# The first stage of a hybrid encoder step: another order of loads, norm steps, weight splits and first dense products

## The chip, the cores and the metric

The kernel runs on one core of a Trainium2 chip. The metric is the device time of one execution in microseconds (us). The engines are named as in the profile: PE (TensorE matmul), PEld (its weight loads), DVE (VectorE), ACT (ScalarE), POOL (GpSimd) and SP (SyncE, which issues most transfers).

## The reference

One layer of a streaming encoder is computed for two request groups that share all weights: 1024 prompt rows and 32 sample rows, here laid side by side as T = 1056 columns. Cut to what matters here:

```
h = rms_norm(x, g_pre_mix)                   # over D_MODEL = 1024
z = h @ w_in                                 # GLA q,k,v,r,rank | band q,k,v | gates gA,gB
... two branches, mixed, w_out, ConvFFN ...
gate = sigmoid(rms_norm(x, g_pre_ple) @ w_ple_gate)
x = x + rms_norm(gate * (pe @ w_ple), g_post_ple)
```

The product pe @ w_ple (called PLE below) does not depend on anything else, so the kernel computes it first, while x is still being loaded and normalised.

## The kernel before, in words

All matrices lie with features on the 128 partitions: x is eight blocks of 128 x 1056, loaded as four parts of two blocks each and two column halves, `one` (columns 0 to 527) and `two` (528 to 1055). Every fp32 product is made from three passes over values split in a high and a low part (hi*hi, hi*lo, lo*hi). A split is an ACT copy to the rounded type (hi) and a subtraction (lo).

The program is written out by hand up to the end of the first stage (`manual_schedule`): PE, DVE and ACT each run their instructions in the order in which the code emits them, and an instruction that waits holds all that stands behind it on its engine. SP issues its transfers in the order of its queue in the same way. The stages that matter:

- **Warm-up and loads** (L311 to L355). The first half of the PLE weights, the three column chunks of p (352 columns each), the small vector table, the four parts of half `one` of x, the second half of the PLE weights, the four parts of half `two`, then `war` and `state_conv`.
- **PLE** (the loop over `PLE`, L443 to L463). 24 groups of six matmuls of 352 columns (L230 to L232): three column tiles for each chunk, then five further tiles. After each group the previous one is copied out of PSUM (`evac`, L457 on ACT; the middle chunk by DVE, L455); after the last chunk of a tile SP writes the tile to DRAM (L459, `d_pl`). There are six PSUM buffers for the groups and four SBUF buffers `ev` for the tiles. The table `S` says which steps of the norm are emitted after which group.
- **Norm of a half** (`x_square`, `x_add`, `x_sums`, `x_inverse`, `x_norm`, `x_low`). ACT squares each part (L363, L366), DVE adds the squares up and folds them (L371, L373, L375), two fp32 matmuls with a constant matrix sum over partitions (L382), ACT takes ln and exp (L385, L386), DVE finishes the reciprocal root (L391 to L395), and then, for each part, DVE scales x (L400), ACT makes the high part xh (L401) and DVE the low part xl (L405).
- **First plain products** (`plain_half`, L469 to L483, and `alr_half`). The band q, k and v tiles and a 48-column rank tile, first for half `one`, then for half `two`: eight k steps of six matmuls of 264 columns each (L475 to L477). The weights' low parts are made by POOL (L331 with `eng=po`, L415). Hooks in the first product emit the sums of half `two`.
- **Sums for the dense pairs** (`sum_differences`, `sum_high`, `sum_low`). Differences of x's blocks for the Strassen-like products, made by DVE (L529 to L531, L540) and ACT (L537) while half `two` is multiplied.
- **Dense pairs** (`in_strassen`). Each pair of output tiles is made of seven products of 24 matmuls (L615 to L617) into three PSUM pairs X, Y, Z. The first product goes to X and is copied to `p1` (L626); weight sums come from DVE (L598) and are split by ACT and DVE (L605, L606). From here on the order is chosen by a scheduler.

Everything behind the dense pairs (band attention, linear recurrence, output product, ConvFFN, gate) follows on PE without a gap of its own order; the change does not touch it, and the order there is the same before and after on every engine.

## Time and profile before

| what | us |
|---|---|
| median of three runs | 1961.51 (1960.55 to 1961.64) |
| the profiled execution | 1960.96 |
| its span | 1959.2 |
| first matmul of PLE | 5.23 |
| sums of half one on PE | 21.52 |
| sums of half two on PE | 51.53 |
| first matmul of the first dense pair | 89.87 |

The span is the time from the first to the last instruction, and the profiled execution took 1.76 us more. A row of the timeline gives the start, the duration, the engine, the line and the tiles; in square brackets stands how long the engine was idle before, and which instruction released it. A row of the windows gives, for a stretch of time, the busy time of PE, PEld, DVE, ACT and POOL with the count of instructions, then the granted clock of PE, the busy share of the DMA engines and the GB/s that they moved. Matmuls overlap, so the pace of PE is read from start to start, not from durations.

### The profile page before, as it was taken

What the parts mean: (1) busy time and instruction counts of PE and PEld (TensorE: products, weight loads), DVE (VectorE), ACT (ScalarE), POOL (GpSimd) and SP (SyncE); (2) the same over time, 40 slices, a digit from 0 to 9 for tenths busy, and PEclk for the clock granted to TensorE, in tenths of its full rate; (3) what the DMA queues carried; (4) which work ended last, traced back from release to release, by engine and by line L of the source; (5) the groups of instructions that cost most, each with busy time, mean ns of one, the idle gap of its engine ahead of it and who ended that gap; (6) DMA issues with size and microseconds to landing.
All of it is one profiled execution on the core that took longest, in us unless ns stands there. A gap on an engine that the chain in (4) does not pass through costs nothing.

```text
span 1959.2 us, 34930 instructions
## 1 busy us (share of the span) xinstructions
PE 1901.6 (97%) x13960; PEld 1863.5 (95%) x13960; DVE 1286.2 (66%) x2368; ACT 929.1 (47%) x1812; POOL 219.6 (11%) x359
## 2 busy tenths in 40 slices
PE   7999999999999999999999999999999999999996
PEld 7999999998999999998999999999999999999996
DVE  6855544556556777778544586777767766558776
ACT  6434334666664454443333455433333345555555
POOL 1100001000000101000320111111121211000112
PEclk9999999999999999999999999999999999999998
DMA  6233325233315455567834245543354559897746
GB/s 257 88 105 100 110 87 181 70 90 88 93 47 144 141 132 155 139 180 218 326 132 126 89 154 196 191 145 127 112 135 110 119 142 308 267 296 240 239 155 106
DMA packets 111120, 300.91 MB, mean 154 GB/s; under 512 B 12453, under 2 KB 34797, under 8 KB 110317
## 3 DMA queue, kind: packets, MB, share of 16 engines
q1 hardware_dynamic: 82652, 210.28, 33.8%
q0 software_dynamic: 28016, 88.05, 16.7%
q8 instruction: 109, 1.79, 0.4%
q14 instruction: 55, 0.44, 0.1%
q10 hardware_dynamic: 288, 0.36, 0.1%
HBM read 201.20 MB, written 114.09 MB: 161 GB/s over the span
## 4 chain that ended last, share of the span: by engine, by line
PE 75%; DVE 13%; ACT 7%; issue 3%; DMA 1%; POOL 0%; SPq 0%; ACTq 0%; DVEq 0%; POOLq 0%
PE two L1903 6%; PE two L1905 6%; PE two L1904 6%; PE mm L230 5%; PE mm L232 5%; PE mm L231 5%; PE mm L796 4%; PE mm L798 4%; PE mm L797 4%; PE two L615 4%; PE two L617 3%; PE two L616 3%; PE two L2350 3%; PE two L2349 3%; PE two L2348 3%
## 5 line engine op out<-in xcount | busy, mean ns | idle before, releaser
L796 PE MATMUL mm<-xh,whi 128*128 128x352 f32 x696 | 236.6, 340 | 0.0
L798 PE MATMUL mm<-xh,wlo 128*128 128x352 f32 x696 | 225.4, 324 | 0.0
L797 PE MATMUL mm<-xl,whi 128*128 128x352 f32 x696 | 224.6, 323 | 0.0
L2350 PE MATMUL two<-d,wlo 128*128 128x264 f32 x616 | 175.5, 285 | 1.2 <-DVE wlo L2092 1.2
L2349 PE MATMUL two<-d,whi 128*128 128x264 f32 x616 | 174.7, 284 | 2.0 <-DVE d L2043 2.0
L2348 PE MATMUL two<-d,whi 128*128 128x264 f32 x616 | 174.7, 284 | 0.8 <-ACT d L2042 0.8
L1905 PE MATMUL two<-mh,wlo 128*128 128x264 f32 x576 | 163.0, 284 | 0.0
L1904 PE MATMUL two<-ml,whi 128*128 128x264 f32 x576 | 162.9, 284 | 0.0
L1903 PE MATMUL two<-mh,whi 128*128 128x264 f32 x576 | 161.2, 284 | 0.0
L796 PEld LDWEIGHTS mm<-xh,whi 128*128 128x128 f32 x696 | 131.3, 189 | 1.7
L797 PEld LDWEIGHTS mm<-xl,whi 128*128 128x128 f32 x696 | 131.2, 189 | 0.4
L798 PEld LDWEIGHTS mm<-xh,wlo 128*128 128x128 f32 x696 | 130.5, 187 | 0.0
L2349 PEld LDWEIGHTS two<-d,whi 128*128 128x128 f32 x616 | 115.8, 188 | 2.4 <-DVE d L2043 2.4
L2348 PEld LDWEIGHTS two<-d,whi 128*128 128x128 f32 x616 | 116.4, 189 | 1.1 <-ACT d L2042 1.1
L2350 PEld LDWEIGHTS two<-d,wlo 128*128 128x128 f32 x616 | 115.6, 188 | 1.6 <-DVE wlo L2092 1.6
L1905 PEld LDWEIGHTS two<-mh,wlo 128*128 128x128 f32 x576 | 108.4, 188 | 0.0
L1904 PEld LDWEIGHTS two<-ml,whi 128*128 128x128 f32 x576 | 108.4, 188 | 0.0
L1903 PEld LDWEIGHTS two<-mh,whi 128*128 128x128 f32 x576 | 107.3, 188 | 0.0
L932 ACT ACTIVATE s<-s,sm 128x640 f32<-128x640 f32 (+5 forms) x72 | 50.6, 703 | 97.1 <-DVE sm L931 97.0
L615 PE MATMUL two<-th,whi 128*128 128x264 f32 x320 | 91.0, 284 | 0.0
L1893 ACT ACTIVATE whi<-ws 128x512 fp32r<-128x512 f32 x72 | 45.2, 631 | 96.4 <-PE two L1904 71.4
L616 PE MATMUL two<-tl,whi 128*128 128x264 f32 x320 | 90.9, 284 | 0.0
(610 smaller groups left out, 6009.2 us busy)
## 6 DMA issues: line engine op xcount, KB each, us to landing
raw<-in_w_in SPq DMA_DIRECT2D x52, 512.0 KB, 3.8
uraw<-d_b SPq DMA_DIRECT2D x34, 528.0 KB, 4.7
d_b<-av POOLq DMA_DIRECT2D x33, 528.0 KB, 4.0
d_ws<-in_w_down POOLq DMA_DIRECT2D x24, 704.0 KB, 6.5
raw<-in_w_up SPq DMA_DIRECT2D x27, 512.0 KB, 3.7
wraw<-d_ws SPq DMA_DIRECT2D x16, 704.0 KB, 6.5
d_b<-gc POOLq DMA_DIRECT2D x11, 792.0 KB, 5.0
sraw<-in_w_up SPq DMA_DIRECT2D x17, 512.0 KB, 4.7
```

Of the source, the lines that this page charges most:

```text
L230: pe.matmul(ps, h, xh(kt), start=(first and i == 0), stop=False)
L615: pe.matmul(ps[:, j, :HC], w[0][:, k], x[0](k, s), start=st, stop=False, skip_group_check=True)
L616: pe.matmul(ps[:, j, :HC], w[0][:, k], x[1](k, s), start=False, stop=False, skip_group_check=True)
L796: pe.matmul(ps, wh, h[:, k, s], start=(k == 0), stop=False)
L797: pe.matmul(ps, wh, l[:, k, s], start=False, stop=False)
L798: pe.matmul(ps, wl, h[:, k, s], start=False, stop=(k == cnt - 1))
L1903: pe.matmul(ps[:, j, :HC], w[0][:, k], x[0][:, k, s], start=st, stop=False, skip_group_check=True)
L1904: pe.matmul(ps[:, j, :HC], w[0][:, k], x[1][:, k, s], start=False, stop=False, skip_group_check=True)
L1905: pe.matmul(ps[:, j, :HC], w[1][:, k], x[0][:, k, s], start=False, stop=sp_, skip_group_check=True)
L2348: pe.matmul(o, wh, xh_[:, s], start=(k == 0 and p in (0, 4, 5)), stop=False, skip_group_check=True)
L2349: pe.matmul(o, wh, xl_[:, s], start=False, stop=False, skip_group_check=True)
L2350: pe.matmul(o, wl, xh_[:, s], start=False, stop=(k == HD - 1 and p in (3, 4, 6)), skip_group_check=True)
```

## The change

Five things change in the first stage.

1. **Loads.** The parts of x's half `one` are loaded between the parts of p. The first w_in tile (QB0) is loaded ahead of half `two`.
2. **Norm steps.** The table `S` is laid out anew, x_norm and the copy to xh are separate steps (`x_norm`, `x_high`), and the steps of half `two` are spread over the three plain products by a table `N`.
3. **No POOL splits.** All low parts of weights come from DVE. All 24 PSUM copies of PLE go to ACT, and the eight writes of PLE tiles (`d_pl`) are issued by ACT and no longer by SP. Two tiles use a buffer of their own (`z`).
4. **Half two** multiplies its tiles in the order 2, 0, 1, and the sums for the dense pairs are emitted in another order.
5. **First dense pair.** Its weights are loaded and the two that need no sum (a11, a12) are split during half `two`; the pair then starts with a11*b11 and a12*b21, both into X.

```
-    x_load(one)
+    x_load(one, 0)
     for c in (1, 2):
         for kt in range(2):
             dma.dma_start(pin[:, kt, chunk(c)], a["p"][kt, :, chunk(c)])
+        x_load(one, 2 * c)
+    x_load(one, 6)
...
-            acc[h.start] = tl(st, [P, 2, HT], tag="acc", bufs=2)
+            acc[h.start] = tl(st, [P, 2, HT], tag="acc", bufs=1)
...
-            wfirst[n] = next(raw_split(raws[n], eng=po))
+            wfirst[n] = next(raw_split(raws[n]))
...
-        po.tensor_tensor(l, raws[n], h, op=ALU.subtract)
+        ve.tensor_tensor(l, raws[n], h, op=ALU.subtract)
...
+    first_load(0)
+    for i in range(0, KT, 2):
+        x_load(two, i)
...
-         9: [lambda: x_square(one, 3)], 10: [lambda: x_add(one, 3), lambda: x_sums(one)],
+         9: [lambda: x_add(one, 3)], 10: [lambda: wple.append(next(raw_split(raws[1]))), lambda: first_load(1)], 11: [lambda: x_sums(one)],
...
-                zs[n] = evt()
-            if c == 1:
-                ve.tensor_copy(zs[n][:, s], ps)
-            else:
-                ac.activation(zs[n][:, s], ps, AF.Copy)
+                zs[n] = tl(st, [P, T], tag="z", bufs=1) if n % 5 == 1 else evt()
+            ac.activation(zs[n][:, s], ps, AF.Copy)
             if c == NC - 1:
-                dma.dma_start(d_pl[n], zs[n])
+                ac.dma_start(d_pl[n], zs[n])
...
+    N = {(0, 0): [lambda: x_low(one, 3), alr_weights, lambda: x_square(two, 3)], (0, 2): [lambda: x_add(two, 2), lambda: first_split(3)],
+         (0, 4): [lambda: x_add(two, 3)], (1, 0): [lambda: first_split(4)], (1, 1): [lambda: x_sums(two)],
...
+    def early_split(n, b):
+        early[n] = [tl(wp, [P, HK, P], F32R, tag=t, bufs=4) for t in ("whi", "wlo")]
+        split_hi_lo(*early[n], early["raw"][0][:, b])
...
+    for i, n in enumerate((2, 0, 1)):
+        plain_half(n, two, sum_hook(i))
     alr_half(two)
+    early_split("a12", up2)
+    sum_low(0, 1)
...
-        mul(X, weight(a11), "b11", True, True)
+        mul(X, early.pop("a11", None) or weight(a11), "b11", True, True)
         ac.activation(p1, X_, AF.Copy)
+        lead = early.pop("a12", None)
+        if lead:
+            mul(X, lead, "b21", False, True)
+            ac.activation(c11, X_, AF.Copy)
```

Where it moves instructions. ACT's queue of before, from the copy of the third PLE group to the ln of half one (`ev` are PLE tiles, `sq` squares of x, `whi` the high part of the second PLE weights; waits in brackets):

```order
L457 ACTIVATE ev_219<-mm_201 128x352
L363 ACTIVATE acc_229<-xr_113 128x1056
L366 ACTIVATE sq_239<-xr_114 128x1056
L457 ACTIVATE ev_195<-mm_241 128x352
L366 ACTIVATE sq_259<-xr_113 128x1056
L330 ACTIVATE whi_261<-raw_151 128x512
L330 ACTIVATE whi_265<-raw_151 128x512
L457 ACTIVATE ev_208<-mm_250 128x352
L457 ACTIVATE ev_219<-mm_271 128x352
L366 ACTIVATE sq_290<-xr_114 128x1056
L457 ACTIVATE ev_299<-mm_281 128x352
L385 ACTIVATE y_303<-one_304 128x264
```

ACT's queue of the changed kernel from the square of x's last part of half one on:

```order
L363 ACTIVATE sq_262<-xr_114 128x1056 [waits DMAHW5_49,DVE_49]
L458 ACTIVATE z_206<-mm_252 128x352 [waits PE_49]
L460 DMA d_pl_88<-z_206 128x1056 [waits DMAHW0_49,Activation_49]
L458 ACTIVATE ev_217<-mm_264 128x352 [waits PE_49]
L460 DMA d_pl_88<-ev_217 128x1056 [waits DMAHW1_49,Activation_49]
L458 ACTIVATE ev_291<-mm_273 128x352 [waits PE_49]
L330 ACTIVATE whi_293<-raw_151 128x512
L330 ACTIVATE whi_297<-raw_151 128x512
L458 ACTIVATE ev_291<-mm_284 128x352 [waits PE_49]
L382 ACTIVATE y_311<-one_312 128x264 [waits PE_49]
```

The writes of PLE tiles now stand in ACT's own queue. The kernel has eight semaphores for SP's and ACT's transfers (DMAHW0 to DMAHW7), given out in turn, so each write waits for the transfer that had the semaphore eight transfers earlier. A little further on in the same queue, behind exp:

```order
L458 ACTIVATE ev_291<-mm_303 128x352
L460 DMA d_pl_88<-ev_291 128x1056 [waits DMAHW3_49,Activation_49]
L360 ACTIVATE acc_328<-xr_113 128x1056 [waits DVE_49]
L458 ACTIVATE ev_337<-mm_319 128x352 [waits PE_49]
L458 ACTIVATE ev_337<-mm_330 128x352 [waits PE_49]
L363 ACTIVATE sq_354<-xr_114 128x1056 [waits DMAHW2_49]
L458 ACTIVATE ev_337<-mm_344 128x352 [waits PE_49]
L460 DMA d_pl_88<-ev_337 128x1056 [waits DMAHW4_49,Activation_49]
L400 ACTIVATE xh_111<-xr_113 128x2x528 [waits DVE_49]
```

DMAHW3 and DMAHW4 are the semaphores of the third and fourth part of x's half `two`; the first high part xh stands behind both writes. On PE, the start of the first dense pair in the changed kernel (`whi_860` is a11, `whi_947` is a12, `two_974` is X; the rows left out repeat the three passes):

```order
L618 MATMUL two_974<-xh_111,whi_860 128x264 [waits DVE_49]
L619 MATMUL two_974<-xl_112,whi_860 128x264
L620 MATMUL two_974<-xh_111,wlo_861 128x264
...
L618 MATMUL two_974<-xh_111,whi_947 128x264 [waits Activation_49]
L619 MATMUL two_974<-xl_112,whi_947 128x264
L620 MATMUL two_974<-xh_111,wlo_948 128x264 [waits DVE_49]
...
L618 MATMUL two_1029<-th_778,whi_1030 128x264 [waits Activation_49]
```

Before, the second product there was the one with `th` and a summed weight; now a second product into X follows the first.

## The prediction

> **What bounds the kernel now.** I read the page first, then the waits of PE in the first 260 us, the windows of ten microseconds there, the windows around PE's slow stretches, and last the timeline row by row.

> ```profile
> span 1959.2 us, 34930 instructions
> ...
> PE 1901.6 (97%) x13960; PEld 1863.5 (95%) x13960; DVE 1286.2 (66%) x2368; ACT 929.1 (47%) x1812; POOL 219.6 (11%) x359
> ```

> PE is busy 97% of the span, so only a stage in which PE waits or runs slowly can give much. The first stage is one: all PE waits of the first 260 us lie ahead of the first dense pair.

> ```profile
> PE one L382 <- DVE acc L375: 4.9, 1, 4.9
> PE mm L477 <- POOL wlo L331: 1.6, 1, 1.6
> PE two L615 <- DVE ev L495: 1.3, 1, 1.3
> PE mm L475 <- ACT whi L330: 1.2, 1, 1.2
> PE mm L476 <- DVE xl L405: 0.9, 1, 0.9
> PE mm L230 <- ACT ev L457: 0.8, 1, 0.8
> ```

> Next to the waits stands a second loss. PE's clock falls to half after two long idle stretches (columns: busy PE, PEld, DVE, ACT, POOL, then the granted clock):

> ```profile
> 18.37:21.79 3.42, 0.27 (x1) 0.28 (x2) 2.50 (x3) 1.21 (x2) 1.24 (x2) 1.00 1.07 387
> 21.50:25.20 3.70, 3.68 (x11) 3.28 (x12) 1.03 (x2) 1.42 (x3) 0.00 (x0) 0.54 1.04 416
> 45.68:49.10 3.42, 0.60 (x3) 0.30 (x2) 3.28 (x3) 3.30 (x6) 2.06 (x2) 1.00 0.20 79
> 49.10:52.50 3.40, 3.33 (x13) 3.13 (x14) 0.58 (x1) 0.00 (x0) 3.40 (x3) 0.50 0.16 28
> 605.00:607.50 2.50, 0.46 (x6) 0.35 (x4) 2.50 (x8) 0.00 (x0) 0.70 (x2) 1.00 0.53 215
> ```

> After 3.4 us that are nearly or wholly idle, 3.4 us follow at 0.50; a single gap of about 2 us (605 to 607) leaves the clock at 1.00. A slow stretch doubles the time of its matmuls, some 1.6 us each time.

> So the measure is when PE passes three places: the sums of half one, the sums of half two, and the first dense product.

> ```profile
> 21.52 1.92 PE L382 MATMUL one<-acc,onesM 128*128 128x264 f32 x4 [4.95 <-DVE acc L375]
> 51.53 1.53 PE L382 MATMUL one<-acc,onesM 128*128 128x264 f32 x4
> 89.87 0.39 PE L615 MATMUL two<-xh,whi 128*128 128x264 f32 x1 [1.26 <-DVE ev L495]
> ```

> Between the second and the third PE has no wait but the last 1.3, before and after, so a lead at 51.53 is carried to 89.87, and from there to the end: behind the first dense pair every engine's order is the same, and PE is the bound.

> **Sums of half one: 21.52 becomes about 20.0.** The fourth part of x has the same transfers ahead of it as before (first PLE weights, p, three parts), so it lands as before: the load of QB0 waited for it and was issued at 15.16. What changes is ACT's queue ahead of its square.

> ```profile
> 15.16 0.33 SPq L320 DMA_DIRECT2D raw<-in_w_in  x1
> 12.26 1.09 ACT L366 ACTIVATE sq<-xr 128x1056 f32<-128x1056 f32 x1 [0.27 <-DMA xr<-in_x]
> 16.40 1.15 ACT L330 ACTIVATE whi<-raw 128x512 fp32r<-128x512 f32 x2 [1.63 <-DMA raw<-in_w_ple]
> 8.79 0.80 ACT L457 ACTIVATE ev<-mm 128x352 f32<-128x352 f32 x2
> 0.81 0.42 ACTq L313 DMA_DIRECT2D pin<-in_p  x1
> 1.35 0.36 ACTq L313 DMA_DIRECT2D pin<-in_p  x1
> 8.65 0.32 PE L230 MATMUL mm<-ph,whi 128*128 128x352 f32 x1
> 9.61 0.33 PE L230 MATMUL mm<-ph,whi 128*128 128x352 f32 x1
> 19.26 1.46 DVE L373 TENSOR_TENSOR acc<-acc,sq 128x1056 f32<-128x1056 f32 x1 [3.20 <-ACT sq L366]
> 20.75 0.71 DVE L375 TENSOR_TENSOR acc<-acc 128x528 f32<-128x528 f32 x1
> ```

> The last chunk of p now has two parts of x ahead of it, as much as the second part had before (12.26), so ACT ends its split at about 12.5. Then come two squares (1.0 each), four copies (0.37 each from start to start) and the first write, which waits for the second PLE weights (landed 16.40; the same bytes stand ahead) and takes 0.42 to issue: 16.8. The last square ends at 17.9, DVE's add and fold at 20.0. PE has 12 groups done instead of 11 and has waited under 2 us, so the clock stays at 1.00.

> The middle chunk of p comes later as well, by one part of x, and PE reaches it at 8.65 (its groups take 0.97, 8.65 to 9.61); the wait of up to 0.7 us there and at the third chunk is paid out of PE's wait for the sums.

> **Sums of half two: 51.53 becomes about 45.8.** Here DVE is the chain. ACT still has two writes, three copies and the split of the second PLE weights (1.15) ahead of ln; the second write waits for QB0 and the third for the first part of half two, some 19.3, so exp ends at about 23.0. DVE's work from there to the fold of half two, from start to start:

> ```profile
> 24.57 0.71 DVE L391 TENSOR_TENSOR rs<-y 128x528 f32<-128x528 f32 x1 [2.67 <-ACT y L386]
> 26.86 1.45 DVE L400 SCALAR_TENSOR_TENSOR xr<-xr,vec,rs 128x528 f32<-128x528 f32 x2
> 28.23 0.51 DVE L455 COPY ev<-mm 128x352 f32<-128x352 f32 x1
> 30.63 3.51 DVE L400 SCALAR_TENSOR_TENSOR xr<-xr,vec,rs 128x528 f32<-128x528 f32 x2
> 30.02 3.56 POOL L331 TENSOR_TENSOR wlo<-raw,whi 128x512 fp32r<-128x512 f32 x2 [10.41 <-ACT whi L330]
> L405 DVE TENSOR_TENSOR xl<-xr,xh 128x1056 fp32r<-128x1056 f32 x8 | 10.0, 1258 | 2.4 <-ACT xh L401 2.4
> L606 DVE TENSOR_TENSOR wlo<-raw,whi 128x512 fp32r<-128x512 f32 x4 | 2.8, 689 | 2.9 <-ACT whi L605 2.9
> ```

> The inverse takes 2.3 (24.57 to 26.86), four norm steps 1.37 each (26.86 to 28.23) = 5.5, four low parts 1.18 = 4.7, three adds of 1.26 = 3.8, four half splits of 0.65 = 2.6, the rank weights 0.65, the fold 0.71: 20.3. The norm step of 3.51 ran beside POOL's splits (30.02 to 33.58); without them I take 1.45. So 43.3 without waits.

> The waits are ACT's. Behind exp the fourth write waits for the third part of half two, and the first xh stands behind that. How ACT's writes and SP's loads share the transfer engines no row shows, so I bound it:

> ```profile
> SPq L459 <- DMA xr<-in_x: 1.8, 2, 0.9
> 20.51 0.33 SPq L320 DMA_DIRECT2D raw<-in_w_in  x1
> L401 ACT ACTIVATE xh<-xr 128x1056 fp32r<-128x1056 f32 x8 | 8.7, 1088 | 13.6 <-DVE xr L400 13.6
> ```

> The first row shows that such waits of a write for a load are real: SP had them before, where they held nothing. The load at 20.51 waited for that third part. QB0 ahead of it costs 1.3 (0.5 MB at some 0.4 MB/us): 21.8 if the writes take nothing, and three writes of 0.53 MB all ahead cost another 4: 25.8. I take 24.4, a bit above the middle, since both queues then have work. [...]

> From 24.4: issue 0.4, square 1.0, two copies 0.74, square 1.0, copy 0.37, issue 0.4, xh 1.09: 29.4. DVE, ready at 28.0, waits 1.4. The split of QB0 follows on ACT after two copies, the second xh and its own 0.6, at 31.7, and DVE (low part done at 30.6) waits 1.1. Together 45.8. PE gets there earlier: by its own work at about 40 (21.1, 12 groups of 0.97, 60 matmuls at 84 in 10 us), plus some 4 of waits on the way (a PSUM copy behind the third xh, a low part). These are covered by the wait for the fold, as a slow stretch of the clock would mostly be.

> **First dense product: 89.87 becomes about 83.7.** The lead is 5.7, and the 0.4 that the slow clock took behind 51.53 comes on top: 6.15. DVE has from 45.8 on the VB0 split 1.3, inverse and norm 12.5, sums for the pairs 17.5, two splits and the rank adds, 34 of 37 us, so PE isn't held.

> **The first pair gives back 0.7.** Its second product goes into X and must wait until p1 is copied.

> ```profile
> 94.33 0.61 ACT L626 ACTIVATE p<-two 128x528 f32<-128x528 f32 x1
> ```

> Before, the copy came 1.3 us after PE had gone on. Now PE ends the first product, drains 0.3, waits 0.61 and two hand-overs: about 1.0, less the 0.3 of hesitations that stood there before. ACT and DVE prepare the third product's weight meanwhile: its sum is ready 7.0 us after the end of the rank tile (DVE: 2.35 for the last `tl`, 1.25 for the rank tile's low part, sums of 0.68), and needed at 8.6.

> **Sum.** 6.15 - 0.7 = 5.45. The same walk over the kernel before, with its order and its slow stretches, ends 1.1 us short of 89.87; hand-overs that I leave out. I charge 0.8: **4.6 us gain**. From the profiled 1960.96 that is 1956.4; the median of the three runs lies 0.55 above the profiled one, and I keep 1956.4.

> **The rivals.**
> - *ACT is not held.* Half two lands before ACT comes to its writes, as if they took no bandwidth. Then the 2.5 of waits and some of the 0.8 go: gain about 8, 1953. Against it: the third part can't land before 21.8, and the writes are large. 0.17.
> - *ACT is held longer.* The third part lands at 25.8, and an issue costs ACT 0.55 as the two at the start lie apart (0.81 and 1.35): 1.4 + 0.9 more in the chain, gain 2.0 to 2.5, 1958.7. 0.22.
> - *The change doesn't do what it says:* p comes so late that PE waits there what it saves at the sums. The bound is the 0.7 twice, and the sums hide it; it decides only from 2 us on. Counted within the case before.
> - *Slower.* DVE takes POOL's splits (six of 0.69, one of 1.3, less eight copies of 0.52) and becomes the bound in half two. Its slack from 45.8 to the pair is 2 to 3 us, and 1.6 more lie ahead of the third product. If DVE is late by more than about 8.5, slower than before. For it: DVE was busy at 9.2 to 9.9 of 10 between 60 and 100 us.

> ```profile
> 60.00:70.00 10.00, 10.00 (x84) 9.99 (x83) 9.27 (x12) 4.37 (x9) 0.00 (x0) 1.00 0.01 2
> 80.00:90.00 10.00, 8.74 (x73) 8.46 (x72) 9.93 (x9) 5.53 (x9) 0.99 (x1) 1.00 0.42 114
> ```

> Against it: PE was the one that set the pace in these rows, and nothing there grows by more than 2 us. A gap of 3.4 us would also bring the slow clock, 1.6 more, so it would come out between 1963 and 1967. 0.10.

> **How the numbers follow.** Forecast 0.51, not held 0.17, held longer 0.22, slower 0.10. The forecast's own bounds (24.4 plus or minus 1.4, the 0.8 from 0 to 1.1, the pair from 0.3 to 1.2) are 1954.5 to 1958.3. The range takes in both neighbours: 1952.6 to 1959.8. A measurement of this kernel tells about 0.2%, 3.9 us, from no change: faster by more means below 1957.6. That is the first rival and some four fifths of the forecast: 0.58. Slower by more, above 1965.4, is some half of the last rival: 0.06. The rest, 0.36, is within.

> **What would show it.** Right: one wait of PE at the sums of half one under 2.5 us and no clock below 1.00 behind it; sums of half two at 45 to 47, waiting for DVE's fold; a write on ACT's queue that waits for a load of x between 22 and 25, and xh behind it; a wait of about 1 us for L629 ahead of the second dense product; no POOL before the memset. Wrong: the fold done before PE comes (then PE's work is the bound and the gain larger), a slow clock behind 36 that is not covered, or a wait of PE for tl, wlo or ws in the first pair.

## The result and the profile after

| | median us | lowest to highest | runs |
|---|---|---|---|
| before | 1961.58 | 1958.83 to 1963.53 | 6 |
| after | 1953.19 | 1952.19 to 1955.88 | 6 |

The ratio is 0.9959, 95% interval 0.9947 to 0.9972: 8.4 us faster, and the interval excludes no change. Predicted were 1956.4, in a range of 1952.6 to 1959.8, so the median lies 0.6 above the range's lower end. The profiled execution took 1952.56, its span is 1950.6. The page after, first lines:

```profile
span 1950.6 us, 34919 instructions
...
PE 1898.7 (97%) x13960; PEld 1861.5 (95%) x13960; DVE 1284.8 (66%) x2367; ACT 931.5 (48%) x1820; POOL 208.0 (11%) x352
```

PE and DVE are busy as long as before within 3 us; the gain is waiting. The waits of PE in the first 260 us after (line, releaser, us in total, times, longest):

```profile
PE one L379 <- DVE acc L372: 1.8, 2, 1.0
PE mm L475 <- ACT z L458: 1.7, 1, 1.7
PE mm L311 <- POOL onesM L168: 1.1, 1, 1.1
PE two L618 <- DVE ev L495: 1.0, 1, 1.0
PE mm L230 <- ACT ph L235: 1.0, 2, 0.7
PE two L618 <- ACT p L629: 0.8, 1, 0.8
```

The 4.9 at the sums of half one is now 1.0, and the sums of half two, where PE came behind the fold before, wait 0.8 for it; the waits for POOL's low parts are gone, and two waits are new: 1.7 for a PSUM copy and 0.8 for the copy of p1. The three places on PE, and the start of the pair's second product, from the timeline after:

```profile
19.58 1.16 PE L379 MATMUL one<-acc,onesM 128*128 128x264 f32 x4 [0.97 <-DVE acc L372]
44.59 1.16 PE L379 MATMUL one<-acc,onesM 128*128 128x264 f32 x4 [0.84 <-DVE acc L372]
82.32 0.39 PE L618 MATMUL two<-xh,whi 128*128 128x264 f32 x1 [1.03 <-DVE ev L495]
86.26 0.39 PE L618 MATMUL two<-xh,whi 128*128 128x264 f32 x1 [0.75 <-ACT p L629]
```

PE leads the kernel before by 1.94, 6.94 and 7.55 us at the three places, and by 7.0 when the first pair is done. DVE's last instruction of the program starts 7.75 earlier (1942.56 against 1950.31), and the span is 8.6 shorter. So seven of the eight microseconds come from the first stage; what is known of the rest stands at "Behind the stage" further down.

### The profile page after: what moved, and what is told of

It reads as the page before. It is cut to its first block, busy times and chain, and to the rows that moved or that the text cites. A ratio compares the mean times of both kernels' runs of the same rounds, so it can differ in the third digit from the quotient of the medians.

```text
span 1950.6 us, 34919 instructions
## 1 busy us (share of the span) xinstructions
PE 1898.7 (97%) x13960; PEld 1861.5 (95%) x13960; DVE 1284.8 (66%) x2367; ACT 931.5 (48%) x1820; POOL 208.0 (11%) x352
## 4 chain that ended last, share of the span: by engine, by line
PE 76%; DVE 12%; ACT 7%; issue 2%; DMA 2%; ACTq 0%; SPq 0%; DVEq 0%
PE two L1911 6%; PE two L1913 6%; PE two L1912 6%; PE mm L230 5%; PE mm L232 5%; PE mm L231 5%; PE mm L804 4%; PE mm L805 4%; PE mm L806 4%; PE two L2358 4%; PE two L2357 4%; PE two L618 4%; PE two L619 3%; PE two L2356 3%; PE two L620 3%
```

## The experiments

Twelve kernels, read at the same places on PE. In e3, e6, e11 and e12 no edit touches what PE does up to the first dense product, so with the profile after there are five profiles of one code. The table gives the places of each profile and the time beside the kernel before on the same chip.

| kernel | sums two | first dense | median us | ratio, 95% |
|---|---|---|---|---|
| before | 51.53 | 89.87 | 1961.58 | |
| after | 44.59 | 82.32 | 1953.19 | 0.9959, 0.9947 to 0.9972 |
| e11 same again | 43.09 | 80.76 | 1953.59 | 0.9961, 0.9948 to 0.9974 |
| e12 fill | 44.07 | 81.81 | 1953.45 | 0.9962, 0.9949 to 0.9974 |
| e6 lead psum | 44.05 | 81.73 | 1953.98 | 0.9959, 0.9945 to 0.9974 |
| e3 pair order | 44.31 | 82.00 | 1957.72 | 0.9982, 0.9973 to 0.9991 |
| e1 pool splits | 44.86 | 82.54 | 1954.89 | 0.9964, 0.9953 to 0.9975 |
| e8 loads back | 45.24 | 82.96 | 1955.38 | 0.9971, 0.9958 to 0.9984 |
| e9 e1 and e8 | 45.01 | 82.72 | 1955.18 | 0.9972, 0.9959 to 0.9985 |
| e14 copies on DVE | 44.79 | 82.47 | 1954.84 | 0.9964, 0.9950 to 0.9978 |
| e15 steps merged | 47.32 | 85.00 | 1957.31 | 0.9975, 0.9965 to 0.9984 |
| e16 e9, e14 and e15 | 49.77 | 87.49 | 1960.92 | 0.9987, 0.9978 to 0.9997 |
| e2 writes on SP | 42.25 | 79.97 | 1951.65 | 0.9951, 0.9936 to 0.9967 |
| e13 e2, e6 and e12 | 42.22 | 79.95 | 1952.78 | 0.9956, 0.9942 to 0.9971 |

The five profiles of one code give 80.76 to 82.32 at the first dense product, mean 81.72. A difference under about 0.8 us there is no finding. Of the kernel before there is one profile, so its own scatter isn't known. The kernel before had a median of 1962.69 beside e6, e14, e15 and e16 and of 1961.1 to 1961.2 beside the other experiments, so those four are compared by ratio.

DVE's chain shows more than PE's places. It runs from the start of half one's inverse (`rs<-y`) to the end of half two's fold, and what DVE doesn't wait there for ACT counts as work:

| kernel | starts | works | waits for ACT | fold ends |
|---|---|---|---|---|
| before | 24.57 | 22.70 | 2.41 | 49.68 |
| after | 22.24 | 19.88 | 2.41 | 44.53 |
| e3, e6, e11, e12 | 21.66 to 22.59 | 19.87 to 19.88 | 1.50 to 2.39 | 43.03 to 44.26 |
| e1 | 22.70 | 21.92 | 0.19 | 44.81 |
| e8 | 23.41 | 19.87 | 1.91 | 45.19 |
| e9 | 21.88 | 21.94 | 1.13 | 44.95 |
| e14 | 21.91 | 21.41 | 1.42 | 44.74 |
| e15 | 21.90 | 19.95 | 5.42 | 47.27 |
| e16 | 23.00 | 23.83 | 2.89 | 49.72 |
| e2 | 21.59 | 19.79 | 0.82 | 42.20 |

One code does the same work each time; what scatters is when the chain starts and how long DVE waits for the first high part. From before to after the fold ends 5.15 earlier: 2.33 by the start, 2.82 by less work, nothing by less waiting. The other 1.8 of the 6.94 at the sums of half two is PE's: before, it came there 1.85 behind the fold, now 0.06.

**e1: the low parts of four first weights on POOL again.**

```
-            wfirst[n] = next(raw_split(raws[n]))
+            wfirst[n] = next(raw_split(raws[n], eng=po))
...
-        ve.tensor_tensor(l, raws[n], h, op=ALU.subtract)
+        po.tensor_tensor(l, raws[n], h, op=ALU.subtract)
...
-10: [lambda: wple.append(next(raw_split(raws[1]))),
+10: [lambda: wple.append(next(raw_split(raws[1], eng=po))),
```

> The changed kernel with the low parts of the second PLE weights and of QB0, KB0, VB0 made by POOL again. In the changed kernel PE reaches the sums of half one at 19.58, those of half two at 44.59 and the first dense product at 82.32. Theory (POOL's splits are slow, 1.7 us a half against 0.65, and slow DVE down beside them, as the norm step of 3.51 against 1.45 in the kernel before): the second PLE weights are 1 us late at 21, DVE's chain to the fold loses 2.6 of its own splits but gains 2 to 4 from slowed steps, and half one's second product waits 1 to 2 us for POOL at 46 to 48; first dense product at 84 to 86, half or more of the gain of the stage back. Rival (the splits are only moved, what they cost DVE they saved on POOL): within 0.7 us of 82.3.

DVE's steps in e1 that run beside POOL's low parts, then these low parts:

```profile
30.83 2.34 DVE L404 TENSOR_TENSOR xl<-xr,xh 128x1056 fp32r<-128x1056 f32 x1
33.09 2.35 DVE L368 SCALAR_TENSOR_TENSOR acc<-sq,acc 128x1056 f32<-128x1056 f32 x1
39.60 3.51 DVE L370 TENSOR_TENSOR acc<-acc,sq 128x1056 f32<-128x1056 f32 x2
43.14 1.67 DVE L372 TENSOR_TENSOR acc<-acc 128x528 f32<-128x528 f32 x1
...
30.54 3.79 POOL L331 TENSOR_TENSOR wlo<-raw,whi 128x512 fp32r<-128x512 f32 x2 [7.38 <-ACT whi L330]
40.72 3.52 POOL L331 TENSOR_TENSOR wlo<-raw,whi 128x512 fp32r<-128x512 f32 x2 [6.39 <-ACT whi L330]
```

In the kernel after, these steps take 1.25, 1.25, 2.5 and 0.71. Beside POOL they lose 4.2 us, while DVE saves two splits of 1.28: with the inverse, 0.3 longer, it works 2.0 more (21.92 against 19.88). Nearly all of that is covered, since DVE waits only 0.19 for ACT: QB0's split is no longer its own, and the fourth write goes as soon as its copy is done. (That holds in e9 and e16 too, where the fifth write is held in its place, 1.2 us; so the edit also changes which write is held.) From its start to the fold's end the chain takes 22.11, and 21.37 to 22.29 in the five profiles. The first dense product at 82.54 is 0.8 above their mean because the chain starts late, and no split of POOL's stands ahead of that start. So the rival holds: the time hardly tells whether POOL or DVE makes the splits.

**e8: half one of x loaded behind p and vec again.**

```
-    x_load(one, 0)
     for c in (1, 2):
         for kt in range(2):
             dma.dma_start(pin[:, kt, chunk(c)], a["p"][kt, :, chunk(c)])
-        x_load(one, 2 * c)
-    x_load(one, 6)
     dma.dma_start(vec, a["vec"])
+    for i in range(0, KT, 2):
+        x_load(one, i)
```

> The changed kernel with half one of x loaded behind p and the vector table, as before; all else as changed. Theory (the fourth part of x has the same bytes ahead of it in either order, and what moved the sums was ACT's queue, in which the last square no longer stands behind the split of the second PLE weights): PE's wait of 0.7 at the middle chunk of p goes, the sums of half one stay at 19.2 to 20.0, half two's and the first dense product within 0.5 of 44.6 and 82.3, same time. Rival (the order of loads is what starts the squares early): sums of half one 1 us or more later, 20.6 to 21.5, and the later places by as much.

The sums of half one stand at 20.75 instead of 19.58 (19.09 to 19.93 in the five profiles), those of half two at 45.24, the first dense product at 82.96: 1.2 later than the mean of the five. That is the rival, and the load order would be worth about a microsecond, little above the scatter. Of the two other kernels with this order, e16 repeats it (20.70) and e9 doesn't (19.35), so it stays open.

**e9: e1 and e8 together** (both diffs above).

> The changed kernel with two of its parts taken back together: half one of x is loaded behind p and vec again, and POOL makes the low parts of the four first weights again. What stays is the order of the norm steps, the copies out of PSUM on ACT and the first dense pair's order. Alone, taking back the loads cost 0.6 us at the first dense product (82.96 against 82.32) and POOL 0.2 (82.54). Theory one: the order of the norm steps carries the gain, and the two parts add: first dense product at 83.0 to 83.5, time about 1955. Rival: each of the two covers for the other, so that both together cost what the change was said to bring by them, several us: first dense product at 86 or later, time 1957.5 or more.

First dense product 82.72: both together cost 1.0, so the rival, that each covers for the other, is out. With these two parts alone taken back, some 7 of the 8 us remain; that the order of the norm steps carries them is not shown by this run.

**e14: the middle chunk of each PLE product copied by DVE again.**

```
-            ac.activation(zs[n][:, s], ps, AF.Copy)
+            if c == 1:
+                ve.tensor_copy(zs[n][:, s], ps)
+            else:
+                ac.activation(zs[n][:, s], ps, AF.Copy)
```

> The changed kernel with the middle chunk of every PLE product copied out of PSUM by DVE again, as before, so that DVE has six copies of 0.45 us (2.7 us) more between the sums of the two halves and ACT six less. Theory one: DVE is the chain up to the fold of half two (PE waits 1.0 for it at 44.59), so every copy counts: sums of half two 2 to 2.7 us later than in the unedited kernel (46.6 to 47.3 against 44.59, 43.09 and 44.07), time about 1955.5. Rival: ACT is the chain (DVE waits for ACT's high parts), so copies taken from ACT give back what they cost on DVE: sums of half two within 0.7 us, time within 1 us of 1953.4.

The sums of half two stand at 44.79 and the first dense product at 82.47, as the rival has it. Five copies came onto DVE between the two sums, four of them in the chain, and DVE works 1.5 longer there. But the high part behind the held write now comes with 1.27 of waiting and QB0's with 0.15, where the kernel after has 1.47 and 0.94. ACT stands so near to DVE in this chain that a copy may lie on either.

**e15: each high part right behind its norm step, the next norm step behind the low part.**

```
-         15: [lambda: x_high(one, 0), lambda: x_norm(one, 1)], 16: [lambda: x_low(one, 0)], 17: [lambda: x_high(one, 1), lambda: first_split(2), lambda: first_load(2)],
-         18: [lambda: x_norm(one, 2)], 19: [lambda: x_low(one, 1), lambda: x_high(one, 2)], 20: [lambda: x_add(two, 1), lambda: x_square(two, 2)],
-         21: [lambda: x_norm(one, 3)], 22: [lambda: x_low(one, 2), lambda: x_high(one, 3)]}
+         15: [lambda: x_high(one, 0)], 16: [lambda: x_low(one, 0), lambda: x_norm(one, 1), lambda: x_high(one, 1)], 17: [lambda: first_split(2), lambda: first_load(2)],
+         19: [lambda: x_low(one, 1), lambda: x_norm(one, 2), lambda: x_high(one, 2)], 20: [lambda: x_add(two, 1), lambda: x_square(two, 2)],
+         22: [lambda: x_low(one, 2), lambda: x_norm(one, 3), lambda: x_high(one, 3)]}
```

> The changed kernel with each norm step followed at once by its high part on ACT, and the next norm step only behind the low part, as before; all else as changed. In the kernel before DVE waited 0.25 and three times 0.72 us for such a high part, and once the norm step is behind the low part ACT's split and copies can't run beside it. Theory one: taking norm steps ahead of the low parts is worth those waits: sums of half two 2 to 3 us later (46.5 to 47.5), time about 1955.5. Rival: it is worth nothing because DVE has other work to put into those waits and PE's wait of 1.0 takes the rest: sums of half two within 0.7 us of the unedited kernel, time within 1 us of 1953.4.

DVE's waits from 22 us to the sums, in the kernel after and then in e15:

```profile
DVE xl L404 <- ACT xh L400: 1.5, 1, 1.5
DVE wlo L331 <- ACT whi L330: 0.9, 1, 0.9
DVE rs L388 <- ACT y L383: 0.8, 1, 0.8
```

```profile
DVE xl L404 <- ACT xh L400: 3.4, 2, 2.2
DVE wlo L331 <- ACT whi L330: 2.0, 1, 2.0
DVE rs L388 <- ACT y L383: 0.8, 1, 0.8
```

DVE works as long as in the kernel after (19.95 against 19.88) and waits 3.0 us more, and the first dense product is 3.3 later than the mean of the five (85.00). Of the four parts this one costs most when it alone is taken back: a norm step done ahead of the low part gives ACT its input early, and the hand-over to ACT and back is hidden.

**e16: e9, e14 and e15 together.**

> The changed kernel with four parts taken back together: load order, POOL's low parts, the middle copies on DVE, and norm steps merged. What stays changed in the PLE stage is the writes on ACT and the places of the squares and adds, and behind it the order of half two's steps and the first dense pair. Theory one: these four carry nearly all of the 7 us, each covering part of another: sums of half two at 50 us or later, first dense product at 88 or later, time 1959 to 1961. Rival: the places of squares and adds, of which half two's now run ahead of the sums, carry half or more: sums of half two at 47 to 48.5, time 1956 to 1957.5.

First dense product 87.49 and a ratio of 0.9987: 5.8 of the 8.15 us are gone (89.87 less the mean 81.72). That lies between the two theories, nearer to the first. Together the parts cost more than singly (1.0, 0.75 and 3.3 make 5.0). DVE's fold and PE's waits ahead of the sums of half two, in the kernel before and then in e16:

```profile
48.02 1.66 DVE L375 TENSOR_TENSOR acc<-acc 128x528 f32<-128x528 f32 x1
47.02 0.39 PE L475 MATMUL mm<-xh,whi 128*128 128x264 f32 x1 [1.24 <-ACT whi L330]
49.17 0.59 PE L477 MATMUL mm<-xh,wlo 128*128 128x264 f32 x1 [1.65 <-POOL wlo L331]
```

```profile
48.05 1.67 DVE L371 TENSOR_TENSOR acc<-acc 128x528 f32<-128x528 f32 x1
46.95 0.39 PE L479 MATMUL mm<-xh,wlo 128*128 128x264 f32 x1 [0.93 <-POOL wlo L331]
49.77 1.16 PE L378 MATMUL one<-acc,onesM 128*128 128x264 f32 x4 [1.33 <-DVE acc L371]
```

The fold is back where it was, so these four parts carry all that DVE's chain gained. What e16 keeps of the gain is PE's: before, PE waited for the high and low part of the second product's weights, ran at half clock behind that and passed the sums 1.85 after the fold; in e16 it waits there for the fold. That is 1.8 of the 2.4 that are left. The other 0.6 lies between the sums and the first dense product: half clock at the sums (49.07 to 52.49), and a wait of 1.26 instead of 1.02 at the end. Which of the kept parts spares PE these waits wasn't tried. The writes on ACT hardly do, since the next run shows that they cost time.

**e2: the writes of PLE tiles issued by SP again.**

```
-                ac.dma_start(d_pl[n], zs[n])
+                dma.dma_start(d_pl[n], zs[n])
```

> The changed kernel with the eight writes of PLE tiles issued by SP again; the copies stay on ACT. Theory (ACT is held by its writes: it waited 0.9 us for a semaphore at 22.6, spends 0.37 on each issue, and DVE then waits 1.47 for the first xh and 0.94 for the split of QB0): these waits of DVE go, the fold of half two is done some 2 us earlier, sums of half two at 42 to 43, first dense product at 79.8 to 80.8, time 2 us under the changed kernel's. Rival (ACT is bound by its own copies and squares, or SP's loads now wait behind the writes as they did before): sums of half two within 0.7 us of 44.6 and the same time.

The fourth write and the first high part behind it on ACT, and DVE's low part that needs it, from the timelines of the kernel after, of e11 (same code) and of e2:

```profile
23.43 0.33 ACTq L460 DMA_DIRECT2D d_pl<-ev  x1
27.70 1.08 ACT L400 ACTIVATE xh<-xr 128x1056 fp32r<-128x1056 f32 x1 [0.77 <-DVE xr L397]
28.81 1.26 DVE L404 TENSOR_TENSOR xl<-xr,xh 128x1056 fp32r<-128x1056 f32 x1 [1.47 <-ACT xh L400]
```

```profile
22.30 0.33 ACTq L460 DMA_DIRECT2D d_pl<-ev  x1
26.20 1.09 ACT L400 ACTIVATE xh<-xr 128x1056 fp32r<-128x1056 f32 x1 [0.40 <-ACT ev L458]
27.32 1.26 DVE L404 TENSOR_TENSOR xl<-xr,xh 128x1056 fp32r<-128x1056 f32 x1 [0.56 <-ACT xh L400]
```

```profile
25.37 1.09 ACT L400 ACTIVATE xh<-xr 128x1056 fp32r<-128x1056 f32 x1 [0.45 <-DVE xr L397]
26.61 1.25 DVE L404 TENSOR_TENSOR xl<-xr,xh 128x1056 fp32r<-128x1056 f32 x1
```

With the writes on SP this wait of DVE goes (the one for QB0's split stays, 0.82), and the first dense product comes at 79.97, 1.75 earlier than the mean of the five; e13, with the same edit among others, has 79.95. The waits are SP's then, where they hold nothing that is late:

```profile
SPq L460 <- DMA xr<-in_x: 2.6, 3, 1.0
```

This shows the predicted mechanism: a write on ACT held by a load of x. The third part of x's half two landed at 23.35 in the kernel after and at 22.23 in e11, and the write went 0.08 behind it. So it also shows the scatter of one code, and all behind the write moved along (sums of half two 44.59 and 43.09). The median of 1951.65 is the lowest of all, but the intervals of e2 and of the kernel after overlap. So this part of the change costs time at the first dense product.

**e3: the first dense pair in the old order** (the second product needs a summed weight again).

```
-    early_split("a12", up2)
```

> The changed kernel with the first dense pair in the order of before: a12 isn't split early and its product stands fourth again; a11 is still split early and the pair's weights still loaded early. First dense product as in the changed kernel (82.3). Theory (the leading second product covers the time that DVE needs for the weight sums, which stand behind 3.6 us of other work): PE waits 2.5 to 3.5 us for the third weight's split behind the first product, where the changed kernel waits 0.75 for the copy of p1; the pair ends 2 to 3 us later and the time is 2 us longer. Rival (the scheduler or DVE gets the sums done within the first product, as in the kernel before): wait under 0.8, time the same or 0.7 shorter.

PE at the second product of e3, and the windows around it (busy PE, PEld, DVE, ACT, POOL, granted clock, DMA share, GB/s):

```profile
87.66 0.39 PE L617 MATMUL two<-th,whi 128*128 128x264 f32 x1 [2.47 <-ACT whi L607]
```

```profile
84.90:88.31 3.41, 0.92 (x6) 0.50 (x5) 3.25 (x6) 1.95 (x4) 0.73 (x1) 1.00 0.29 78
88.31:91.72 3.41, 3.41 (x16) 3.41 (x17) 3.03 (x6) 0.85 (x2) 0.00 (x0) 0.50 0.20 62
```

The wait of 2.5 brings a slow stretch on top in this profile; against e12 PE is 3.75 late behind the pair, where it came to the pair 0.2 late. The cause is DVE: the first sum for the second product starts at 85.52, 3.5 us behind the pair's start, since a low part of `tl` (2.34) and the rank tile's (1.25) now stand ahead of it. Before, it started at 89.74, with the pair. So the new pair doesn't give back: it covers what the new order of the sums puts behind the rank tile.

**e6: the second leading product in a PSUM pair of its own.**

```
-            mul(X, lead, "b21", False, True)
-            ac.activation(c11, X_, AF.Copy)
+            W = ps_pair()
+            mul(W, lead, "b21", True, True)
+            ve.tensor_tensor(c11, p1, W[:, :, :HC], op=ALU.add)
```

> The changed kernel with one edit in the dense pairs that are led by two products: the second product goes into a PSUM pair of its own and DVE adds p1 to it, where the unedited kernel adds on top of p1's pair and so waits for the copy of p1 on ACT (0.75 us at the second dense product). If the wait is what the pair gives back, as predicted, it goes: second product 0.7 us earlier behind the first (3.2 instead of 3.9 us), and PE holds that lead at 110 us: time 0.7 under 1953.4. Rival: the sums for the third product are late then, so PE waits there for what it saved: the same at 110 us and the same time.

The wait for p1 is gone, and PE is 0.97 ahead of e12 inside the second product. Then it waits 0.28 for a high part, and later for a low part that stands behind DVE's added sum: at 89.3 the lead is -0.03, from 90 on -0.13. The rival holds: the wait was not what set the end of the pair, DVE's sums were.

**e11: the changed kernel once more, unedited.**

> The changed kernel once more, nothing edited. In the six profiles so far each slow stretch of PE's clock lasts 3.41 us, two in one profile lie a whole multiple of 3.41 us apart, and the place of this grid differs from profile to profile (remainders 1.3, 0.6, 3.3, 0.1, 3.0, 3.4 us). Theory one: the grid runs by itself and a gap brings a slow stretch only if one of its windows is less than about half busy; then this profile has another remainder, and the stretches at 34.7 us and near 600 us can appear or vanish with the same code: near 600 us a stretch and a span 1.7 us longer, or none. Rival: the code sets the places: a stretch at 34.7 us again, none near 600 us, span 1950.6 within 0.5.

The grid's remainder (the start of a slow stretch, less whole multiples of 3.413 us) is 2.99 here, by the one stretch of this profile, at 1938.35, and was 0.60. There is no slow stretch at 34 us and none near 600. Of the 34 us stretch in the kernel after and in e14, and of two more in e14, the windows before and in the stretch:

```profile
31.32:34.73 3.41, 1.74 (x10) 1.38 (x9) 3.41 (x5) 2.03 (x5) 0.00 (x0) 1.00 0.60 190
34.73:38.14 3.41, 2.95 (x13) 2.95 (x14) 3.41 (x5) 2.94 (x6) 0.00 (x0) 0.50 0.57 227
```

```profile
31.43:34.84 3.41, 1.59 (x11) 1.38 (x10) 3.41 (x6) 2.18 (x3) 0.00 (x0) 1.00 0.81 255
34.84:38.25 3.41, 3.41 (x16) 3.41 (x17) 3.41 (x4) 2.16 (x5) 0.00 (x0) 0.50 0.54 221
598.04:601.45 3.41, 1.36 (x10) 1.25 (x10) 3.41 (x11) 0.74 (x4) 0.76 (x2) 1.00 0.41 161
601.45:604.86 3.41, 3.41 (x16) 3.41 (x15) 0.61 (x2) 1.25 (x7) 0.31 (x1) 0.50 0.69 211
1615.21:1618.62 3.41, 1.61 (x11) 1.40 (x11) 1.98 (x4) 0.62 (x2) 1.85 (x2) 1.00 1.02 401
1618.62:1622.03 3.41, 3.18 (x13) 2.88 (x14) 1.68 (x3) 3.10 (x5) 0.00 (x0) 0.50 0.88 252
```

The starts 34.84, 601.45 and 1618.62 are all 0.70 above a multiple of 3.4133. Theory one holds: the same code meets the grid at different places. The five profiles of one code have the remainders 0.60, 0.83, 1.50, 2.98 and 2.99. The span of 1950.0 is 0.6 under that of the kernel after, by the first theory's "none" and just outside the rival's 0.5; it has little weight here.

**e12: PE kept busy in its wait near 599 us.** The first two products of the first head are made four times instead of once, so this kernel does more work than needed.

```
-        for n, o, w in ns:
+        for n, o, w in ns * (4 if u == 0 else 1):
             pe.matmul(dg[:w, o : o + w], k[:, n * P : n * P + w], q[:, n * P : n * P + w], start=True, stop=True)
```

> The changed kernel with the first head's first products (two matmuls into dg) made four times instead of once, the same values into the same place, so PE is busy for some 1.5 us of its wait of 2.0 near 599 us. Theory one (a window less than half busy brings 3.41 us at half clock, 1.7 us lost, by chance of where the grid stands): no slow stretch near 600 us in this profile, the next product at the same 2.0 us after, and the median 0.5 to 1.2 us below that of the unedited kernel beside it, with less spread. Rival (the stretches near 600 us have another cause, or the idle engine is no loss there): median the same within 0.3, or later by the 1.5 us of the added matmuls.

PE's next product in e11 and in e12:

```profile
598.84 0.41 PE L1239 MATMUL one<-ident,x 128*128 128x128 f32 x2 [2.05 <-DVE x L1199]
```

```profile
598.98 0.41 PE L1239 MATMUL one<-ident,x 128*128 128x128 f32 x2 [0.58 <-DVE x L1199]
```

The wait shrinks from 2.05 to 0.58, and the product is 0.14 later, where PE came to the first dense pair 1.05 later. Of twelve profiles without the fill, before included, eight have a slow stretch near 600 us (e1, e2, e3, e8, e9, e14, e15, e16), of the two with it none. But the median is 0.14 under e11's, not 0.5 to 1.2: the gain in time is not shown. One reason shows at 1317 us, where PE loses 1.1 to e11. ACT there in e11 and in e12, and PE's wait in e12:

```profile
1310.08 1.27 ACT L1763 ACTIVATE gc<-gx,vec 128x1058 f32<-128x1058 f32 x1 [2.06 <-DMA d_b<-gc]
1312.39 1.27 ACT L1763 ACTIVATE gc<-gx,vec 128x1058 f32<-128x1058 f32 x1 [4.21 <-DMA d_b<-gc]
1317.65 0.39 PE L1911 MATMUL two<-mh,whi 128*128 128x264 f32 x1 [0.82 <-DVE gx L1923]
```

From the issue of that transfer to ACT's start it is 6.7 us here, 6.4 in e13, which has the fill too, and 4.7 to 5.4 in the twelve profiles without the fill. DVE's `gx` stands behind ACT's step, and PE waits for `gx`. Why the transfer takes longer with the fill is not known.

**e13: e2, e6 and e12 together.**

> The changed kernel with three edits: the writes of the PLE products issued by SP instead of ACT, the second leading product of the first dense pair in a PSUM pair of its own (the third sum is then p1 plus that, added by DVE), and the added products near 597 us. If the gains add: first dense product at 80.0 (2.35 earlier, as with SP's writes alone), the pair 0.7 shorter since PE waits for no copy of p1, and no slow stretch near 600 us: 3.0 us under the unedited kernel with like clock, time about 1949 to 1950.5. Rival: what is gained in the first stage is lost behind the pair, because DVE's added sum or another wait is late, or because PE isn't the bound there: within 1 us of the unedited kernel.

The first dense product comes at 79.95 as expected, but the time is only 0.8 under e11's: within the rival's 1 us. The PSUM pair gives nothing, as in e6, and PE loses another 1.1 us to e11 at 1317 and 1328 us, in both places behind such a transfer. That e13 is better than the changed kernel isn't shown.

## Why the prediction was right, and where it was off

The direction, the range and the mechanism held: DVE's chain ends last at both sums (PE waits for `acc` there), the writes on ACT are held by x, and the lead is carried to the end within about a microsecond (7.0 behind the first pair, 8.1 at 1000 us, 7.8 at the end). The size didn't: the forecast was 3.2 us above the median after, and gave the profiled run a gain of 4.6 where it is 8.4. The median lies outside the forecast's own bounds (1954.5 to 1958.3), at the 1953 of the rival "ACT is not held", and that rival's cause didn't come: the write was held and DVE waited. That the range, widened for the rivals, took the median in by 0.6 is luck. By the prediction's own steps:

- **Sums of half one**: 20.0 predicted, 19.58 measured, no slow stretch behind them. Right.
- **The held write**: DVE's wait for the first high part 1.4 predicted, 1.47 measured; for QB0's 1.1 and 0.94. The sizes agree partly by chance: the first wait is 0.56 to 1.47 in the five profiles, and the write went earlier than predicted, but DVE was ready earlier too. No run shows the 24.4 at which the third part was taken to land: it was the author's estimate between 21.8 and 25.8, and how ACT's writes and SP's loads share the transfer engines was not shown. In the kernel after the part landed at 23.35, and the write it holds went at 23.43, and at 22.30 to 23.53 in the five.
- **The chain to the fold**: exp ended at 22.22, not 23.0: the third write, taken to be held until 19.3, went at 18.75. From there to the fold's end it took 22.3 (44.53), not 22.8, since DVE's work is 19.9 and not 20.3. Together 1.3 us: the sums of half two at 44.59, not 45.8. A slow stretch of the clock came at 34.73 and was covered by the wait for the fold, as predicted.
- **The pair**: gave back 0.55 (lead 7.55 ahead of it, 7.0 behind), not 0.7. The size was right and the reading wrong: e6 shows that DVE's sums set it, and e3 that the old order would have cost 3.6 more.
- **The charge of 0.8** for hand-overs is a term that failed: nothing of it appeared, and PE came to no place later than the walk had it. The walk stood at a lead of 6.15 at the first dense product, and measured is 7.55, the chain's 1.3 and a bit. So the missing 3.8 us are 1.4 of the chain, 0.8 of the charge, 0.15 of the pair, and 1.4 of the next point.
- **Behind the stage** the prediction had nothing; 1.4 us of the profiled difference arise there. 0.7 of it comes near 600 us, where DVE waits for a transfer, before and after:

```profile
603.81 0.71 DVE L1064 TENSOR_TENSOR qo<-qo,kq 128x528 f32<-128x528 f32 x1 [5.99 <-DMA kq<-d_kq]
596.08 0.71 DVE L1072 TENSOR_TENSOR qo<-qo,kq 128x528 f32<-128x528 f32 x1 [5.20 <-DMA kq<-d_kq]
```

  From PE's first product behind the first pair to this step it is 492.9 before and 492.2 after, and 492.1 to 493.0 in the five profiles of one code: chance. 0.85 is the end of the program (from DVE's last instruction to the end of the span 8.2 before, 7.4 after; 7.1 to 8.2 among the experiments), so chance too; 0.2 goes the other way outside the span (the span is 8.6 shorter, the time 8.4). One place behind the pairs is not the same in both kernels: near 760 us SP issues a load of w_in ahead of one of `vt` before, and behind it after. Whether that matters isn't shown; PE's lead grows by 0.3 between 700 and 860 us.
- **The parts that carry it.** The prediction put 2.06 of its sum on POOL's split beside a norm step. DVE's work does shrink by 2.0 without POOL's splits (e1), but nearly all of it would have been covered by waits for ACT. The order of the norm steps, which the walk took as free, costs 3.3 when it alone is taken back. Neither is the gain from before to after by itself: DVE's waits for ACT are 2.41 in both kernels. The parts need each other: with the copies gone from DVE, the old order leaves it waiting 5.42 for ACT (e15), and with the other parts back as well 2.89 (e16).
- **The clock.** That "a single gap of about 2 us (605 to 607) leaves the clock at 1.00" was read from one profile and doesn't hold: the same gap near 600 us was followed by half clock in eight profiles of twelve. Of the kernel before's two stretches in the first stage, the one behind 4.95 us of waiting would come wherever the grid lies. This is an estimate from the 4.95 and the bound of 0.40 in the last section: some window of 3.41 us is then at most some 0.3 busy (measured there: 0.07).

The slower rival didn't come: PE waits 1.0 for DVE ahead of the first pair, about as before (1.3).

## What to carry to other kernels

Where two engines hand a tile back and forth, do the next tile's first step ahead of this tile's last one: here taking that order back cost 3.3 us, more than taking back any of the moves of work between engines. A DMA issued from a computing engine's queue can hold that engine for an unrelated transfer: here the fourth write on ACT went 0.08 us behind a load of x, and with the writes on SP the first dense product came 1.75 us earlier. Look at what it waits for before it is moved there. And before a difference of one or two microseconds is explained, profile the same code twice: five profiles of one code lie 1.56 us apart at the first dense product.
